# Tying TensorE's order in two attention branches of a decoder trunk, with stick-breaking values in pairs

## The chip, the cores and the metric

The kernel runs on one core of a Trainium2 chip. The metric is the device time of one execution in microseconds (us). A core has five engines that matter here: TensorE (PE in the rows, its weight loads PEld), VectorE (DVE), ScalarE (ACT), GpSimd (POOL) and SyncE (SP), which issues DMAs. Each has a queue of its own and works it off in the order in which it was written; semaphores tie the queues together.

## The reference, cut to what matters

One layer of a decoder trunk over 1024 tokens of 1024 channels in float32: a token mixer of three gated attention branches, then a feed-forward network with a short convolution.

```python
def banded_attention(q, k, v, bias, mask):      # branches A and B, per block of 128 queries, 256 keys
    logits = jnp.einsum('nkgbqd,nkbsd->nkgbqs', qb, kw) * SCALE
    logits = jnp.where(mask, logits + bias[:, :, None], -jnp.inf)
    m = jnp.max(logits, axis=-1)
    p = jnp.exp(logits - m[..., None])
    l = jnp.sum(p, axis=-1)
    num = jnp.einsum('nkgbqs,nkbsd->nkgbqd', p, vw)

def stick_breaking_attention(q, k, v):          # branch C, per block of queries
    z = jnp.einsum('bhqd,bhsd->bhqs', q, k) * SCALE
    log_keep = jnp.where(before, jax.nn.log_sigmoid(-z), 0.0)
    log_rest = lax.cumsum(log_keep, axis=3, reverse=True) - log_keep
    wts = jnp.where(before, jnp.exp(jax.nn.log_sigmoid(z) + log_rest), 0.0)
    out = jnp.einsum('bhqs,bhsd->bhqd', wts, v)
...
merged = g0 * (o_a @ w_br_a) + g1 * (o_b @ w_br_b) + g2 * (o_c @ w_br_c)
```

Branch A is dilated: three groups of heads with dilations 1, 4 and 16, whose results are combined per token by their softmax denominators. Branch B is a sliding window with a sink per head.

## The kernel before, in words

The input projection, the feed-forward's first product and its last are done by seven block products instead of eight, with float32 operands split into two parts and three matmuls each (`mm3_steps`, line 133). Between the input projection and the output projection lies the stretch that matters here, from about 578 to 905 us of the profile.

*Banded branches A and B.* `att_AB` (line 805) gives four stages for a pair of query blocks. `scores` (line 812) makes the logits on TensorE (`mm_qk`, lines 719 and 720), VectorE adds the bias and takes the maximum in one reduction (line 826), and ScalarE the exponentials (line 879 for A, 977 for B). `settled` lets ScalarE scale B's probabilities (line 986). `transposed` turns the probabilities on TensorE (line 845) and VectorE copies them out of PSUM (line 847). `values` multiplies them by the values (line 859): outputs of 64 rows, so the matmuls use one half of the array's columns for each head. The loop at line 1150 has 24 rounds; A has 24 pairs of blocks (6 units of 4), B has 16. In round k it traces transposes of A(k), scores of A(k + 2), transposes of B(k), scores of B(k + 2), values of A(k), values of B(k). From k = 16 A is alone. `combine` (line 918) joins A's dilated groups: small VectorE operations, then transposes (line 941) and six broadcast products (line 949) through a PSUM bank with the tag "cum". It runs beside the loop from k = 12 for the first pair of heads.

*Stick-breaking branch C.* `att_C` (line 723) has 40 steps of two heads, 128 keys and up to 256 queries. `logits` of step n + 3 (line 736) are followed by a chain over VectorE, ScalarE and GpSimd (lines 744 to 755). `weights` adds the step to the running sum in the bank "cum" (line 763); VectorE subtracts it (line 764) and ScalarE exponentiates. `carry` (line 771) prepares the sum for the next step; it must wait until VectorE has read. `values` (line 778) makes two 64-column products into the bank "o", and ScalarE copies that out at the end of a group of steps (line 783). In each round the trace has carry(n - 1), weights(n), then a yield, then values(n - 1) and logits(n + 3), then a yield.

At each yield the main loop (line 1172) puts in 11/9 steps of `fill` (three matmuls of line 137 each): the projections of branches B and A by `branch` (line 1011), each with a product by the gate on VectorE (lines 1034 and 1036), and the loads and splits of the output weights. The second `combine` runs beside it, a step at each yield.

*What sets the order.* The program is written with tiles; its scheduler takes the traced instructions and writes each engine's queue from when it expects them to be ready. So a queue is not always in the order of the text. Shared banks set the order too: "d" (three banks) for logits, "z" (two) for transposes and fill, "oab", "o" and "cum" (one each).

Of the kernel before, what the change touches and what calls it, by code (L numbers as in the profile page):

```python
# [72 lines left out]
def decoder_kernel(ctx, tc, x, rel_bias, attn_pre, w_in, b_gate, sinks, w_br_a, w_br_b, w_br_c,  # L73
# [290 lines left out]
    nc.tensor.transpose(ps[:, :KT], grow, ident[:KT, :KT])  # L364
# [12 lines left out]
    def to_channels(grp, k):  # L377
        ps = bank_z("ps_xT")
        for i in range(4):
            nc.tensor.transpose(ps[:, i * P : i * P + P], xts[4 * grp + i][:, k * P : k * P + P], ident)  # L380
        return ps
# [70 lines left out]
    def init_vectors():  # L452
# [14 lines left out]
        for i in range(3):  # L467
            n = 24 if i == 0 else P
            ps = bank_z("ps_vec")
            nc.tensor.transpose(ps[:, :n], vrow[:n, i, :], ident[:n, :n])  # L470
            nc.vector.tensor_copy(pvec[:, i, :n], ps[:, :n])

        nc.vector.memset(table[NBUCKET : NBUCKET + 1, :], 1.0)
        for s in range(4):
            h0, nh = 4 * s, (4 if s < 3 else 8)
            ps = bank_z("ps_rv")
            nc.tensor.matmul(ps[:nh, :384], table[:, h0 : h0 + nh], oh[:, s, :], start=True, stop=True)
# [55 lines left out]
    def keep_v(c, u, r):  # L533
        dil = dil_of(c)
        if T // dil < P:
            by_r = hst["b"][:, r, 1, :]
            nc.scalar.copy(by_r.rearrange("p (r l) -> p r l", r=dil), by_residue(u, dil))
            u, dil = by_r, 1
        v = hst["b"][:, r, 0, :].rearrange("p (i c) -> p i c", i=NB)
        for n in range(2):  # L540
            ps = bank_z("ps_v")
            for i in range(4):
                b = 4 * n + i
                r, l = divmod(b * P, T // dil)
                t0 = dil * l + r
                nc.tensor.transpose(ps[:, i * P : i * P + P], u[:, t0 : t0 + dil * (P - 1) + 1 : dil], ident)
            nc.vector.tensor_copy(v[:, 4 * n : 4 * n + 4, :], ps.rearrange("p (i c) -> p i c", i=4))
        nc.gpsimd.dma_start(v_d[VS.index(c)], v)
# [168 lines left out]
    def mm_qk(z, q, k, kl, ss, ms):  # L717

        nc.tensor.matmul(z, q[:, ss], k[:, ms], start=True, stop=False)
        nc.tensor.matmul(z, q[:, ss], kl[:, ms], start=False, stop=True)  # L720


    def att_C():
# [6 lines left out]
        def logits(n):  # L730
# [3 lines left out]
            for hh in range(2):  # L734
                for m, x in enumerate(("k", "kl")):
                    nc.tensor.matmul(z[:, hh, c0:], uC[p][j // 4][x][hh][:, j % 4 * P : j % 4 * P + P],  # L736
                                     uC[p][c // 2]["q"][hh][:, 256 * (c % 2) + c0 : 256 * (c % 2) + 256],
                                     start=m == 0, stop=m == 1 and j < 2 * c)
                if j >= 2 * c:
                    nc.tensor.matmul(z[:, hh, c0 : c0 + P], negd[:, 0, :], negd[:, 1, :], start=False, stop=True)  # L740
# [17 lines left out]
        def weights(n, p, c, j, c0, z, sp):  # L758
# [3 lines left out]
            for m, part in enumerate(sp):  # L762
                nc.tensor.matmul(cum, Lm, part, start=m == 0 and j == 2 * c + 1, stop=True, skip_group_check=True)
# [4 lines left out]
        def carry(n, p, c, j, c0, z, sp):  # L768
            if j > 0:
                for part in sp:  # L770
                    nc.tensor.matmul(banks["cum"][:, :, c0:], NLm, part, start=False, stop=True, skip_group_check=True)

        def values(n, p, c, j, c0, z, sp, w):
# [3 lines left out]
            for hh in range(2):  # L777
                nc.tensor.matmul(o[HR[hh], c0:256], uC[p][j // 4]["v"][:, j % 4, HR[hh]], w[:, hh], start=(j == 2 * c + 1), stop=(j == 0),  # L778
                                 skip_group_check=True)
# [9 lines left out]
        for n in range(len(steps)):  # L789
# [4 lines left out]
            if n > 0:  # L794
                values(n - 1, *live[n - 1], ws_[n - 1])
# [5 lines left out]
        values(n, *live[n], ws_[n])  # L801
# [3 lines left out]
    def att_AB(u, vcol, bias, banded, own, negm, soften, done, otag):  # L805
# [32 lines left out]
        def transposed(n):  # L838
# [3 lines left out]
            for hh in range(2):  # L842
                ps = psz.tile([P, 4, P], F32, tag="z", name="ps_pT")
                for m, (b, c) in enumerate(slots):
                    nc.tensor.transpose(ps[:, m, :], prs[hh][:, b, c * P : c * P + P], ident)  # L845
# [5 lines left out]
        def values(n):  # L851
# [4 lines left out]
            for m, (b, c) in enumerate(slots):  # L856
                i, nch = 2 * n + b, ws[b] // P
                for hh in range(2):
                    nc.tensor.matmul(o[HR[hh], (i % 4) * P : (i % 4) * P + P],  # L859
                                     u["v"][:, i - (nch - 1) + c, vcol(hh) : vcol(hh) + 64], pTs[hh][:, m, :],  # L860
                                     start=(c == 0), stop=(c == nch - 1))
# [56 lines left out]
    def combine(p):  # L918
# [226 lines left out]

    for k in range(2):
# [28 lines left out]
    for _ in fill:  # L1175
        pass
    raws_c = load_branch(w_br_c)
# [57 lines left out]
    def residual(tt, ys):  # L1235
# [22 lines left out]
        for kh in range(2):  # L1258
            ps = bank_e("ps_hT") if tt == NB - 1 else bank_d("ps_hT")
            for k in range(4):  # L1260
                nc.tensor.transpose(ps[:, k * P : k * P + P], y[:, (4 * kh + k) * P : (4 * kh + k + 1) * P], ident)
# [104 lines left out]
    def down_product(banks, make, start, stagger=0, side=iter(())):  # L1366


        def step(kk, e, hl, ms):
            sh, th = hl  # L1370
            for m in ms:
                for n, (a, b) in enumerate(PASSES):
                    f0 = kk == 0 and e == 0 and n == 0
                    nc.tensor.matmul(banks[m], sh[:, a, m * P : m * P + P], th[:, b], start=start and f0,  # L1374
                                     stop=kk == NK - 2 and e == 1 and n == 2, skip_group_check=not start)
# [173 lines left out]
```

## Time and profile before

| what | value |
|---|---|
| runs (3) | median 1950.8 us, 1949.98 to 1953.85 |
| the profiled execution | 1950.72 us, span 1948.9 us |
| mean granted TensorE clock | 0.991 of full speed |
| TensorE, VectorE, ScalarE, GpSimd busy | 96%, 73%, 52%, 15% of the span |
| chain that ended last | 69% TensorE, 9% VectorE, 9% issue, 7% DMA |

The span goes from the first to the last instruction; the execution's time has 1.8 us more. Busy time is the union of an engine's instructions. TensorE's matmuls overlap one another: each row's duration is longer than the time until the next matmul starts, so what a matmul costs is read from the starts of the timeline. In a row of the timeline, "x4" says that four instructions of one form follow each other; a bracket gives the idle time of the engine before the row and what ended it. A value product appears as two records.

### The profile page before, as it was taken

To read this page: it belongs to the slowest core of one execution; us is meant where nothing else is said; L and a number is where in the kernel's file an instruction comes from. 1 tells how busy PE (TensorE), PEld (TensorE's weight loads), DVE (VectorE), ACT (ScalarE), POOL (GpSimd) and SP (SyncE) were. 2 spreads that over 40 slices of the span, in tenths; PEclk is the share of its full clock that TensorE was granted. 3 is DMA by queue.
4 is the path that set the end of the run, shared out by engine and by line. 5 is a ranking of instruction groups with operands and counts; after the bars stand their busy time and mean duration, and the time that the engine had idled before them with its cause. 6 is when DMAs were issued, how large, how long until landed. Compare 5 with 4: busy or idle time off the path is not lost.

```text
span 1948.9 us, 24575 instructions
## 1 busy us (share of the span) xinstructions
PE 1878.8 (96%) x8904; PEld 1513.3 (78%) x8904; DVE 1425.5 (73%) x2280; ACT 1011.9 (52%) x1903; POOL 292.7 (15%) x333
## 2 busy tenths in 40 slices
PE   6899999999999999999989999999999999999997
PEld 4788887788887766767877888888888888878875
DVE  7866655445538879797588877878787875599896
ACT  6644433344449966773455554545455454445443
POOL 4212200100011003374150000000000000010122
PEclk9999999999999999999999999999999999999999
DMA  4487743643358542344223322222232217686572
GB/s 153 137 232 204 217 129 105 211 151 111 106 209 268 201 150 92 108 128 170 93 71 109 96 76 87 78 85 87 76 97 76 87 55 266 221 315 225 183 261 94
DMA packets 220409, 283.57 MB, mean 146 GB/s; under 512 B 14639, under 2 KB 145725, under 8 KB 220288
## 3 DMA queue, kind: packets, MB, share of 16 engines
q1 hardware_dynamic: 197168, 202.03, 32.2%
q0 software_dynamic: 22960, 79.90, 12.6%
q8 instruction: 70, 1.15, 0.2%
q14 instruction: 51, 0.42, 0.1%
q10 hardware_dynamic: 160, 0.07, 0.0%
HBM read 207.94 MB, written 77.95 MB: 147 GB/s over the span
## 4 chain that ended last, share of the span: by engine, by line
PE 69%; issue 9%; DVE 9%; DMA 7%; ACT 3%; POOL 2%; SPq 0%; DVEq 0%; POOLq 0%; ACTq 0%
PE st_a L137 26%; PE st_c L137 12%; PE e L1374 6%; PE st_b L137 6%; PE ps_y L137 4%; PE d L1374 3%; PE ps_b L137 3%; PE o_ab L859 2%; PE ps_pT L845 1%; DMA rep_d<-rv_d 1%; PE z_c L736 1%; DVE bT L120 1%; DMA rc<-g_d 1%; DMA ra<-g_d 1%; PE o_c L778 1%
## 5 line engine op out<-in xcount | busy, mean ns | idle before, releaser
L137 PE MATMUL st_a<-bT,w_hl 128*128 128x512 f32 x2124 | 514.9, 392 | 9.1 <-DVE mixbuf L128 3.1
L137 PEld LDWEIGHTS st_a<-bT,w_hl 128*128 128x128 f32 x2124 | 401.1, 189 | 96.5 <-DVE mixbuf L128 3.5
L118 ACT ACTIVATE w_hl<-w_raw 128x512 fp32r<-128x512 f32 x236 | 147.4, 630 | 295.6 <-PE st_c L137 171.6
L1374 PE MATMUL e<-th,sh 128*128 128x512 f32 x912 | 216.0, 390 | 2.7 <-DVE th L120 2.6
L118 ACT ACTIVATE w_hl<-s 128x512 fp32r<-128x512 f32 x177 | 111.6, 633 | 195.4 <-PE st_a L137 176.1
L120 DVE TENSOR_TENSOR w_hl<-w_raw,w_hl 128x512 fp32r<-128x512 f32 x236 | 165.7, 705 | 60.3 <-ACT w_hl L118 60.2
L1374 PEld LDWEIGHTS e<-th,sh 128*128 128x128 f32 x912 | 170.9, 188 | 39.9 <-DVE th L120 4.0
L120 DVE TENSOR_TENSOR w_hl<-s,w_hl 128x512 fp32r<-128x512 f32 x177 | 122.9, 696 | 88.4 <-ACT w_hl L118 88.3
L137 PE MATMUL st_a<-b,w_hl 128*128 128x512 f32 x708 | 180.9, 401 | 4.5 <-DVE w_hl L120 4.0
L1325 DVE SCALAR_TENSOR_TENSOR ybuf<-ubuf,pvec,ybuf 128x1023 f32<-128x1023 f32 (+1 forms) x128 | 163.8, 1281 | 21.0 <-ACT ybuf L1323 19.9
L137 PE MATMUL st_b<-b,w_hl 128*128 128x512 f32 x708 | 171.5, 390 | 0.0
L137 PE MATMUL st_c<-bT,w_hl 128*128 128x512 f32 x708 | 170.6, 389 | 0.0
L137 PE MATMUL st_c<-b,w_hl 128*128 128x512 f32 x684 | 164.7, 389 | 0.0
L137 PEld LDWEIGHTS st_a<-b,w_hl 128*128 128x128 f32 x708 | 134.8, 193 | 34.1 <-DVE w_hl L120 4.7
L137 PEld LDWEIGHTS st_c<-bT,w_hl 128*128 128x128 f32 x708 | 133.0, 188 | 27.8 <-ACT w_hl L118 0.2
L137 PEld LDWEIGHTS st_b<-b,w_hl 128*128 128x128 f32 x708 | 132.9, 188 | 27.6
L137 PEld LDWEIGHTS st_c<-b,w_hl 128*128 128x128 f32 x684 | 128.6, 188 | 27.0 <-ACT ubuf L247 0.2
L1374 PE MATMUL d<-th,sh 128*128 128x512 f32 x432 | 107.3, 391 | 3.1 <-DVE th L120 3.0
L137 PE MATMUL ps_b<-o_hl,wb_hl 128*128 128x512 f32 x384 | 105.2, 399 | 4.5 <-DVE gate L1036 2.9
L1330 POOL DMA_DIRECT2D g_d<-ybuf x32 | 17.1, 535 | 591.8 <-DVE ybuf L1329 591.8
L1374 PEld LDWEIGHTS d<-th,sh 128*128 128x128 f32 x432 | 80.7, 188 | 21.9 <-DVE th L120 5.1
L137 PE MATMUL ps_y<-wo,m_hl 128*128 128x512 f32 x384 | 88.8, 391 | 0.0
(273 smaller groups left out, 2934.5 us busy)
## 6 DMA issues: line engine op xcount, KB each, us to landing
w_raw<-in_w_up_dram SPq DMA_DIRECT2D x65, 512.0 KB, 4.2
w_raw<-in_w_in_dram SPq DMA_DIRECT2D x54, 512.0 KB, 5.2
ra<-g_d SPq DMA_DIRECT2D x40, 512.0 KB, 4.5
rb<-in_w_down_dram SPq DMA_DIRECT2D x40, 512.0 KB, 4.8
k_d<-hst POOLq DMA_DIRECT2D x36, 512.0 KB, 7.2
g_d<-ybuf POOLq DMA_DIRECT2D x32, 512.0 KB, 2.9
gate_d<-mixbuf POOLq DMA_DIRECT2D x24, 512.0 KB, 4.4
gate<-gate_d SPq DMA_DIRECT2D x48, 256.0 KB, 3.6
```

The costliest lines, as they stand in the source:

```text
L118: nc.scalar.activation(hi, src, AF.Copy, scale=scale)
L120: nc.vector.tensor_tensor(lo, src, hi.bitcast(F32), op=ALU.subtract)
L137: nc.tensor.matmul(ps, st(a, k), mv(b, k), start=start and n == 0, stop=stop and n == 3 * nk - 1, **kw)
L736: nc.tensor.matmul(z[:, hh, c0:], uC[p][j // 4][x][hh][:, j % 4 * P : j % 4 * P + P], uC[p][c // 2]["q"][hh][:, 256 * (c % 2) + c0 : 256 * ...
L778: nc.tensor.matmul(o[HR[hh], c0:256], uC[p][j // 4]["v"][:, j % 4, HR[hh]], w[:, hh], start=(j == 2 * c + 1), stop=(j == 0), skip_group_ch ...
L845: nc.tensor.transpose(ps[:, m, :], prs[hh][:, b, c * P : c * P + P], ident)
L859: nc.tensor.matmul(o[HR[hh], (i % 4) * P : (i % 4) * P + P], u["v"][:, i - (nch - 1) + c, vcol(hh) : vcol(hh) + 64], pTs[hh][:, m, :], sta ...
L1325: nc.vector.scalar_tensor_tensor(y[:, d:], src[:, : T - d], cw[2 - d][:, c : c + 1], y[:, d:], op0=ALU.mult, op1=ALU.add)
L1330: nc.gpsimd.dma_start(g_d[f * P : f * P + P, :], ys[0])
L1374: nc.tensor.matmul(banks[m], sh[:, a, m * P : m * P + P], th[:, b], start=start and f0, stop=kk == NK - 2 and e == 1 and n == 2, skip_grou ...
```

## The change

Between `ordered = True`, ahead of the first scores of A and B, and `ordered = False`, behind the last fill, each TensorE instruction is tied behind the one that was traced before it on TensorE. No semaphore is added, only the order in the queue is set. In the stick-breaking branch the values of two steps are traced together, in the rounds with even n. The second `combine` uses the bank "oab", which the banded branches leave, in place of "cum".

```diff
+    ordered = False
+
+    def pe(ins):
+
+        return tc.keep_in_program_order(ins) if ordered else ins
...
-                nc.tensor.matmul(ps, st(a, k), mv(b, k), start=start and n == 0, stop=stop and n == 3 * nk - 1, **kw)
+                pe(nc.tensor.matmul(ps, st(a, k), mv(b, k), start=start and n == 0, stop=stop and n == 3 * nk - 1, **kw))
...
@@ -791,14 +797,16 @@
                 carry(n - 1, *live[n - 1])
             ws_.append(weights(n, *live[n]))
             yield
-            if n > 0:
-                values(n - 1, *live[n - 1], ws_[n - 1])
+            if n > 0 and n % 2 == 0:
+                for m in (n - 2, n - 1):
+                    values(m, *live[m], ws_[m])
             if n + 3 < len(steps):
                 live.append(logits(n + 3))
             if steps[n] == (0, 3, 2):
                 load_C(1, 1, uC[1][1])
             yield
-        values(n, *live[n], ws_[n])
+        for m in (n - 1, n):
+            values(m, *live[m], ws_[m])
...
         for n in range(2):
-            ps = pso.tile([P, 512], F32, tag="cum", name="ps_w")
+            ps = pso.tile([P, 512], F32, tag=("cum", "oab")[p], name="ps_w")
             for i in range(4):
-                nc.tensor.transpose(ps[:6, i * P : i * P + P], cg[:, 4 * n + i].rearrange("a g h -> a (g h)"), ident)
+                pe(nc.tensor.transpose(ps[:6, i * P : i * P + P], cg[:, 4 * n + i].rearrange("a g h -> a (g h)"), ident))
...
-                pw = pso.tile([P, 512], F32, tag="cum", name="pw")
-                nc.tensor.matmul(pw, sel[:, g, :], wT, start=True, stop=True)
+                pw = pso.tile([P, 512], F32, tag=("cum", "oab")[p], name="pw")
+                pe(nc.tensor.matmul(pw, sel[:, g, :], wT, start=True, stop=True))
...
+    ordered = True
     for k in range(2):
         sa.scores(k)
         sb.scores(k)
...
     for _ in fill:
         pass
+    ordered = False
     raws_c = load_branch(w_br_c)
```

The same `pe(...)` stands around all other calls on TensorE in these functions (lines 719, 720, 736, 740, 763, 771, 778, 845 and 859). `keep_in_program_order` adds an edge to the queue's previous instruction and returns the instruction. Outside the stretch `pe` returns its argument.

## Rows read from the trace of the kernel before

**Rows 1.** Part 1 of the page: busy time, share, instructions.

```profile
PE 1878.8 (96%) x8904; PEld 1513.3 (78%) x8904; DVE 1425.5 (73%) x2280; ACT 1011.9 (52%) x1903; POOL 292.7 (15%) x333
```

**Rows 2.** Windows: stretch, us; busy PE, PEld, DVE, ACT, POOL; clock, DMA share, GB/s.

```profile
583.00:665.00 82.00, 78.76 (x689) 63.69 (x689) 67.86 (x321) 77.29 (x289) 7.08 (x12) 1.00 0.72 244
665.00:694.00 29.00, 27.99 (x222) 20.31 (x221) 24.89 (x98) 22.73 (x82) 1.43 (x2) 1.00 0.40 136
694.00:717.00 23.00, 22.12 (x193) 17.31 (x190) 19.29 (x83) 15.24 (x57) 1.35 (x2) 1.00 0.63 191
717.00:755.00 38.00, 35.52 (x182) 24.64 (x180) 31.65 (x50) 23.88 (x48) 9.96 (x9) 1.00 0.39 126
755.00:820.00 65.00, 65.00 (x345) 46.33 (x344) 52.90 (x85) 47.94 (x94) 21.57 (x18) 1.00 0.27 87
820.00:881.00 61.00, 56.56 (x273) 36.83 (x271) 59.35 (x79) 41.94 (x77) 43.56 (x30) 1.00 0.44 143
881.00:905.00 24.00, 20.79 (x88) 15.74 (x87) 21.00 (x24) 6.18 (x8) 17.46 (x15) 1.00 0.82 292
```

**Rows 3.** TensorE's timeline in the banded stretch: start, duration, work.

```profile
645.41 1.09 PE L859 MATMUL o_ab<-pT,v 128*64 128x128 f32 x14
646.43 0.39 PE L719 MATMUL z_ab<-b_qk 128*128 128x256 f32 x1
...
646.77 0.29 PE L719 MATMUL z_ab<-b_qk 128*128 128x256 f32 x1
646.90 0.28 PE L720 MATMUL z_ab<-b_qk 128*128 128x256 f32 x1
647.10 0.43 PE L859 MATMUL o_ab<-pT,v 128*64 128x128 f32 x2
647.47 0.33 PE L719 MATMUL z_ab<-qk 128*128 128x128 f32 x1
```

**Rows 4.** The same timeline: first and last of 72 visits of line 859.

```profile
583.81 0.43 PE L859 MATMUL o_ab<-pT,v 128*64 128x128 f32 x2
...
716.06 1.09 PE L859 MATMUL o_ab<-pT,v 128*64 128x128 f32 x14
```

**Rows 5.** TensorE's timeline in the stick-breaking branch.

```profile
772.18 0.65 PE L778 MATMUL o_c<-zs,v 128*64 128x256 f32 x4
772.77 0.73 PE L736 MATMUL z_c<-q,k 128*128 128x256 f32 x4
773.34 0.86 PE L137 MATMUL ps_b<-o_hl,wb_hl 128*128 128x512 f32 x3
774.06 0.50 PE L771 MATMUL cum<-sp,tri 128*128 128x256 f32 x2
...
774.87 0.86 PE L137 MATMUL ps_b<-o_hl,wb_hl 128*128 128x512 f32 x3
775.66 0.44 PE L778 MATMUL o_c<-zs,v 128*64 128x128 f32 x4
776.03 0.74 PE L736 MATMUL z_c<-q,k 128*128 128x256 f32 x4
```

**Rows 6.** Waits (us, times, longest): ScalarE 583 to 665, TensorE 820 to 881.

```profile
ACT o_hl L118 <- PE o_ab L859: 2.4, 5, 1.1
...
PE cum L771 <- DVE zs L125: 1.7, 4, 0.8
```

**Rows 7.** VectorE by line, 694 to 717 us: count, busy, mean ns, idle before.

```profile
L847 DVE COPY pT<-ps_pT 128x256 f32<-128x256 f32 (+2 forms) x15 | 7.7, 544 | 3.0 <-PE ps_pT L845 3.0
L826 DVE CUSTOM_DVE_ANT_0 s_ab<-z_ab,bias 128x256 f32<-128x256 f32 (+1 forms) x24 | 7.5, 363 | 0.0
```

**Rows 8.** TensorE's timeline, 717 to 755 us: rows with idle time.

```profile
722.20 0.50 PE L763 MATMUL cum<-sp,tri 128*128 128x256 f32 x2 [0.67 <-DVE wT L943]
...
725.28 0.50 PE L771 MATMUL cum<-sp,tri 128*128 128x256 f32 x2 [1.18 <-DVE zs L125]
...
744.13 0.60 PE L941 MATMUL ps_w<-ident,cg 128*6 128x128 f32 x4 [0.63 <-DVE zs L125]
```

More of the change, by code (lines that the diff above doesn't have):

```diff
@@ L363, in decoder_kernel @@
     ps = bank_z("ps_g0")
-    nc.tensor.transpose(ps[:, :KT], grow, ident[:KT, :KT])
+    pe(nc.tensor.transpose(ps[:, :KT], grow, ident[:KT, :KT]))
     nc.vector.tensor_copy(g_attn, ps[:, :KT])
@@ L379, in to_channels @@
         for i in range(4):
[L380 removed]
+            pe(nc.tensor.transpose(ps[:, i * P : i * P + P], xts[4 * grp + i][:, k * P : k * P + P], ident))
         return ps
@@ L476, in init_vectors @@
             ps = bank_z("ps_rv")
-            nc.tensor.matmul(ps[:nh, :384], table[:, h0 : h0 + nh], oh[:, s, :], start=True, stop=True)
+            pe(nc.tensor.matmul(ps[:nh, :384], table[:, h0 : h0 + nh], oh[:, s, :], start=True, stop=True))
             rv = buf[:nh, 2560 + 384 * s : 2560 + 384 * s + 384]
@@ L717, in mm_qk @@
     def mm_qk(z, q, k, kl, ss, ms):
-        nc.tensor.matmul(z, q[:, ss], k[:, ms], start=True, stop=False)
-        nc.tensor.matmul(z, q[:, ss], kl[:, ms], start=False, stop=True)
+        pe(nc.tensor.matmul(z, q[:, ss], k[:, ms], start=True, stop=False))
+        pe(nc.tensor.matmul(z, q[:, ss], kl[:, ms], start=False, stop=True))
     def att_C():
@@ L762, in weights @@
             for m, part in enumerate(sp):
-                nc.tensor.matmul(cum, Lm, part, start=m == 0 and j == 2 * c + 1, stop=True, skip_group_check=True)
+                pe(nc.tensor.matmul(cum, Lm, part, start=m == 0 and j == 2 * c + 1, stop=True, skip_group_check=True))
             sub(w, z, cum)
@@ L770, in carry @@
                 for part in sp:
-                    nc.tensor.matmul(banks["cum"][:, :, c0:], NLm, part, start=False, stop=True, skip_group_check=True)
+                    pe(nc.tensor.matmul(banks["cum"][:, :, c0:], NLm, part, start=False, stop=True, skip_group_check=True))
         def values(n, p, c, j, c0, z, sp, w):
@@ L777, in values @@
             for hh in range(2):
-                nc.tensor.matmul(o[HR[hh], c0:256], uC[p][j // 4]["v"][:, j % 4, HR[hh]], w[:, hh], start=(j == 2 * c + 1), stop=(j == 0),
-                                 skip_group_check=True)
+                pe(nc.tensor.matmul(o[HR[hh], c0:256], uC[p][j // 4]["v"][:, j % 4, HR[hh]], w[:, hh], start=(j == 2 * c + 1), stop=(j == 0),
+                                 skip_group_check=True))
             if j == 0:
@@ L858, in values @@
                 for hh in range(2):
-                    nc.tensor.matmul(o[HR[hh], (i % 4) * P : (i % 4) * P + P],
+                    pe(nc.tensor.matmul(o[HR[hh], (i % 4) * P : (i % 4) * P + P],
                                      u["v"][:, i - (nch - 1) + c, vcol(hh) : vcol(hh) + 64], pTs[hh][:, m, :],
-                                     start=(c == 0), stop=(c == nch - 1))
+                                     start=(c == 0), stop=(c == nch - 1)))
             if n % 2 == 1:
@@ L1373, in step @@
                     f0 = kk == 0 and e == 0 and n == 0
-                    nc.tensor.matmul(banks[m], sh[:, a, m * P : m * P + P], th[:, b], start=start and f0,
-                                     stop=kk == NK - 2 and e == 1 and n == 2, skip_group_check=not start)
+                    pe(nc.tensor.matmul(banks[m], sh[:, a, m * P : m * P + P], th[:, b], start=start and f0,
+                                     stop=kk == NK - 2 and e == 1 and n == 2, skip_group_check=not start))
         held = []
```

14 lines of the change are left out of this document (7 added, 7 removed).

## The prediction

> **What bounds the kernel now.** Part 1 of the page comes first: TensorE is busy for 1878.8 of 1948.9 us [rows 1]. A matmul's row is longer than the time until the next may start, so a busy share of 96% does not say that the array is full; for that the starts are needed. Next the stretch that the change touches is cut into seven windows [rows 2]. In the first 82 us of the banded attention ScalarE is busy for 77.29 us, that is 94%: the exponentials and scalings set the pace, and TensorE, at 78.76 us, has little more to spare. From 665 to 694 us, where the first combination of the dilated groups runs beside it, ScalarE falls to 22.73 of 29 us and TensorE is at 27.99. From 694 to 717 us only the dilated branch is left: TensorE 22.12, VectorE 19.29, ScalarE 15.24 of 23. In the stick-breaking branch TensorE has no gap from 755 to 820 us (65.00 of 65), and from 820 to 881 us VectorE is the bound with 59.35 of 61. A saving on TensorE is therefore worth different sums in these windows.
>
> Last the order of TensorE's work is read from its timeline. In the banded stretch the value products (line 859) do not stand together: a visit of two records, then logits, transposes, another visit [rows 3]. From the first to the last of them [rows 4] I count 72 visits: 41 before 665 us, 18 from there to 694 us, 13 after. The text of the program asks for 24 groups: 16 in which both branches' values follow each other, and 8 of the dilated branch alone. In the stick-breaking branch TensorE already runs as the text says: values, logits, fill, carry, weights, fill, values [rows 5]. So tying the order changes much in the first part and little in the second.
>
> **What a visit costs.** Fourteen records take 646.43 - 645.41 = 1.02 us to the next product, two take 647.47 - 647.10 = 0.37 us [rows 3]. That is 0.054 us a record and 0.26 us for the visit itself. Going in costs too: the logits product before a visit holds the engine for 647.10 - 646.90 = 0.20 us, one with logits behind it for 0.13 us, so 0.07 us. A visit costs 0.33 us beyond its work. Changes between transposes and logits I set at nothing, since the one way gains about what the other loses.
>
> **The banded stretch to 694 us.** 59 visits become 16; 43 times 0.33 is 14.2 us of TensorE's time. Not all of it can come back, because ScalarE is next. In the first window ScalarE idles 82 - 77.29 = 4.7 us, and 2.4 us of that is its copy of finished outputs waiting for the last value product [rows 6]; tied order doesn't take that wait away. I take 1 us there. From 665 to 694 us the 18 visits become 4, which is 4.6 us, and ScalarE has 6.3 us to spare; I take 4 us. **Term: -5 us.** Bounds: 4.7 + 4.6 = 9.3 us gained; at the other end 3 us lost, if TensorE waits in its new order for probabilities that ScalarE gives late, by the idle 2.4 us of [rows 6] and a little more.
>
> **The dilated branch alone, 694 to 717 us.** 13 visits become 8, a gain of 1.7 us. Against it stands a new wait. In tied order the queue is transposes(k), scores(k+2), values(k), and values need the copies of both transposed tiles (line 847). Behind the waiting product stands everything of TensorE, the next logits first, on which VectorE and then ScalarE live. A copy takes 0.544 us [rows 7]; two come to 1.1 us, and since the first begins while the second half is still being transposed I take 1 us for both. For k = 16 to 21 eight logits products of 0.13 us [rows 3] cover that, unless VectorE first works off up to four reductions of 0.363 us and their read-outs [rows 7]: 0 to 1.8 us a round; I take 0.3, together 1.8 us. For k = 22 and 23 there are no scores left and nothing covers: 2 us. In the old order the first logits of the stick-breaking branch and its fill stood there. **Term: +2 us.** Bounds: -1.7 with no wait, +11 with all of them (2 + 6 times 1.8 - 1.7).
>
> **The start of the stick-breaking branch.** Before, the second combination borrows the bank of the running sum, and weights wait for it: 0.67 us at 722.20, 1.18 us at 725.28 and 0.63 us at 744.13 [rows 8] are TensorE's whole idle time from 717 to 755 us, 38 - 35.52 = 2.5 us [rows 2]. With the bank "oab" this conflict goes. But the combination's chain is now tied into the queue: each of its six broadcast products needs the bank back from VectorE's multiplication (an estimate of 0.7 us with its hand-over, from the copy's 0.544 us [rows 7]), and its transposes need the small VectorE chain. Also the branch's first logits now start behind the last values, not 8 us before them. **Term: 0**, between -2.5 (idle time gone) and +4.2 (six waits of 0.7 us).
>
> **Values of two steps together.** Full-width values take 772.77 - 772.18 = 0.59 us, half-width 776.03 - 775.66 = 0.37 us [rows 5]; half the columns cost 0.22 us, so 0.59 - 0.44 = 0.15 us is the visit. Going in: three fill products before values take 775.66 - 774.87 = 0.79 us, before a carry 774.06 - 773.34 = 0.72 us. A visit costs 0.22 us, and 20 of 40 go: 4.4 us. Only the window where TensorE is the bound can give it back, some 20 steps between 755 and 820 us, so 10 visits: 2.2 us. After 820 us VectorE's 59.35 us are the same work [rows 2]. The step moves no DMA and no output copy: each pair ends where the single one did, and the logits' buffer that is read longer is refilled only by logits that stand behind in the same queue. What it takes away is cover: in the odd rounds some 0.6 us of values no longer stand between weights and the next carry, which waits for VectorE's subtraction. That wait is 1.7 us in four places now [rows 6]. The even rounds give the same back, so I set it at nothing; if seven odd rounds lose all of it, it is +4 us. **Term: -2 us**, from -4.4 to +2.
>
> [...]
>
> **Sum.** -5 + 2 + 0 - 2 = -5 us. The profiled execution took 1950.72 us (span 1948.9), 0.1 us off the median of 1950.8; the forecast is 1945.7, said as 1946 us. Nothing after 905 us is touched by the diff; I let it shift. About 0.2%, or 3.9 us, is what a measurement of this kernel can tell from no change, so this forecast lies just on the faster side of that line.
>
> **Rivals.** *The wait for the copies decides (slower).* Place: values behind their transposes, in the banded stretch. Price: if both copies lie open in each of 24 groups, 24 times 1.1 us = 26 us, less 48 visits or 15.8 us, less 2 us of the pairs: +8 us, 1959 us. It decides once the open wait passes (15.8 + 2)/24 = 0.74 us a group. For it: the old order broke the values up just where the copies were late, and VectorE works 83% of that stretch [rows 2]. Against it: scores of the same round stand between, and in 16 of 24 rounds those of two branches. [...]
>
> *ScalarE and VectorE hide it (no change).* The banded stretch stays at ScalarE's pace, the lone branch loses 2 us, the pairs give 2: 1950 us. For it: ScalarE's 94% in the first window and VectorE's 97% from 820 us [rows 2]. A form of it is that the tie does nothing in the stick-breaking branch, which already runs so.
>
> *TensorE is the true bound (much faster).* All 15.8 us and 4.4 us come back: 1931 us. Against it: ScalarE has only 11 us idle before 694 us.
>
> **Chances.** The forecast's case has 0.50 (own range 1938 to 1951): 0.32 beyond the line, since its centre lies there and its terms reach further down than up, 0.13 within 0.2%, 0.05 slower. The slower rival has 0.20, all of it slower. No change has 0.20, of which 0.04 for a gain over the line. The much faster case has 0.10. Faster by over 0.2%: 0.32 + 0.04 + 0.10 = 0.46; the same 0.13 + 0.16 = 0.29; slower 0.05 + 0.20 = 0.25. The range goes from 1934 us, which leaves out the far end of the large gain, to 1958 us, just short of the slower rival's middle.
>
> **What would show it.** Right: some 24 value visits in the banded stretch, runs of 32 records, TensorE's sum of busy time there down by over 10 us while ScalarE's share rises over 94%; the stretch shorter by about 5 us to 694; in the stick-breaking branch eight value records in a row, 20 times, and no wait of weights on the combination. The lone branch not shorter. Wrong: value products that wait for pT by over 0.7 us each; carries that wait for VectorE in odd rounds; a gain that is gone by 905 us; or a stretch after 905 us that changes its length.

## The result and the profile after

| | median | lowest to highest | ratio to before, 95% interval |
|---|---|---|---|
| before | 1950.39 us | 1948.01 to 1953.85 | |
| changed | 1963.13 us | 1957.72 to 1964.53 | 1.0056 [1.0041, 1.0070] |

The change makes the kernel slower by half a per cent, outside the range that was given. (The ratio is not the quotient of the two medians, which would be 1.0065.) The profiled execution of the changed kernel took 1957.72 us (span 1955.9), 7.0 us more than the one of before. It is the shortest of the six; the medians are 12.7 us apart, so the 7.0 us that are followed up below are not all of the difference.

Part 1 of the page, which answers to [rows 1]:

```profile
PE 1864.8 (95%) x8904; PEld 1515.9 (78%) x8904; DVE 1427.4 (73%) x2280; ACT 1011.3 (52%) x1903; POOL 292.3 (15%) x333
```

The instructions are the same in number on every engine. TensorE is busy 14 us less and the kernel is longer: time went from work into waiting.

**Where it went.** Four landmarks are read from TensorE's timeline, each by the start of its product: the first banded logits, the last value product of branch B, the last of branch A, and the last of the stick-breaking branch.

| stretch | before | changed | difference | predicted term |
|---|---|---|---|---|
| first banded logits to B's last values | 116.1 us | 121.3 us | +5.2 | -5 |
| from there to A's last values | 22.8 us | 23.8 us | +1.0 | +2 |
| from there to the last stick-breaking values | 163.9 us | 162.5 us | -1.4 | 0 - 2 |

That is +4.8 of the 7.0 us. The rest lies in stages that the diff doesn't touch; the largest part of it is the last product of the feed-forward, 3.2 us longer in this profile. The first stretch is the failure. Its windows, in the changed kernel (columns as in [rows 2]):

```profile
583.00:665.00 82.00, 68.91 (x627) 60.56 (x626) 62.93 (x295) 70.77 (x267) 6.31 (x11) 0.89 0.71 238
583.00:594.00 11.00, 7.38 (x41) 6.30 (x41) 7.25 (x37) 9.68 (x40) 3.50 (x7) 0.66 1.00 362
594.00:612.00 18.00, 16.44 (x159) 14.83 (x157) 13.27 (x64) 15.06 (x57) 0.71 (x1) 0.88 0.72 252
612.00:665.00 53.00, 45.09 (x434) 39.43 (x433) 42.42 (x198) 46.02 (x172) 2.10 (x3) 0.94 0.64 208
```

ScalarE, which set the pace with 77.29 of 82 us [rows 2], is busy for 70.77 now. So nothing came off its work; it is given work too late. And a column that said 1.00 in every row of before says 0.66, 0.88 and 0.94: TensorE was at half clock for part of each window. Cut finer, the granted clock of the changed kernel is 0.50 in whole windows (582 to 584, 589 to 594, 606 to 608, 626 to 629 and 647 to 649 us) and 1.00 between them (595 to 605, 609 to 625, 630 to 645 us). So a mean of 0.66 in 11 us means 11 x 0.34 x 2 = 7.5 us at half clock; with 4.3, 6.4 and another 1.8 us just before 583 that is 20 us. Before, the stretch had none.

What TensorE waited for, from 577 to 723 us (us in all, times, longest):

```profile
PE ps_pT L853 <- ACT pr L994: 13.9, 9, 3.1
PE o_ab L867 <- ACT num L899: 1.5, 2, 0.8
PE ps_pT L853 <- DVE pT L855: 1.4, 2, 0.9
PE z_ab L725 <- DVE st L834: 1.3, 1, 1.3
PE o_ab L867 <- DVE pT L855: 1.1, 4, 0.6
...
```

One line holds most of the waiting: transposes of branch B (line 853, once 845) wait for line 994 (once 986), ScalarE's scaling of B's probabilities in `settled`. The wait for the copies of the transposed tiles, on which the slower rival was built, is the last line shown, 1.1 us.

The longest of these waits on ScalarE's timeline, in the changed kernel (start, duration, work, idle time before):

```profile
587.56 0.51 ACT L985 ACTIVATE pr<-s_ab,nm 128x256 f32<-128x256 f32 x1 [1.32 <-DVE nm L978]
...
589.15 0.49 ACT L985 ACTIVATE pr<-s_ab,nm 128x256 f32<-128x256 f32 x1
...
589.64 1.48 ACT L994 ACTIVATE pr<-pr,l 128x128 f32<-128x128 f32 x4
```

and the same place in the kernel before:

```profile
587.27 0.80 ACT L986 ACTIVATE pr<-pr,l 128x128 f32<-128x128 f32 x2
587.98 0.49 ACT L977 ACTIVATE pr<-s_ab,nm 128x256 f32<-128x256 f32 x1
...
590.04 0.78 ACT L986 ACTIVATE pr<-pr,l 128x128 f32<-128x128 f32 x2
```

In both kernels the scalings of round 0 stand in ScalarE's queue among or behind the exponentials of round 1. Before, two of the four ran at 587.27, and TensorE's queue held other work until the rest were done. In the changed kernel all four stand behind the exponentials, which themselves begin late. TensorE's timeline shows what the tied order does with that:

```profile
586.73 0.28 PE L726 MATMUL z_ab<-k,q 128*128 128x256 f32 x1
590.08 1.78 PE L853 MATMUL ps_pT<-ident,pr 128*128 128x128 f32 x6 [3.07 <-ACT pr L994]
591.51 0.56 PE L725 MATMUL z_ab<-b_qk 128*128 128x256 f32 x1
...
600.85 0.88 PE L853 MATMUL ps_pT<-ident,pr 128*128 128x128 f32 x6
601.48 0.30 PE L725 MATMUL z_ab<-qk 128*128 128x128 f32 x1
```

The transposes of B(0) are at the head of the queue and TensorE stands still for 3.07 us, from 587.01. What the scalings need was there long before they ran: VectorE finished their reciprocals (line 990, also part of `settled`) at 587.61 us.

```profile
587.44 0.17 DVE L990 RECIPROCAL l<-l 128x4 f32<-128x4 f32 x1
```

From there to 589.64 us ScalarE did exponentials that stand ahead in its queue: 2.03 of the 3.07 us are the place of the scalings, the rest is VectorE's reciprocal before and the first scaling behind. Behind the transposes are the logits of B(2), on which VectorE and then ScalarE live, so ScalarE runs dry a round later: its exponentials at 594.81 us wait 0.74 us for a maximum from VectorE, and from 583 to 665 us such waits are 4.5 us in four places, where they were 0.7 us in two before. And the six transposes take 591.51 - 590.08 = 1.43 us to the next product, where six take 601.48 - 600.85 = 0.63 us later; the granted clock is 0.50 from 589 to 594 us and 1.00 from 595 to 605. The half clock came with the wait.

What was predicted of the order itself did happen. The 72 visits of value products [rows 4] are 24 groups, such as 16 + 16 records at 661.79 and 662.72 us. The stick-breaking branch has its pairs (TensorE's timeline, beside [rows 5]):

```profile
776.72 1.08 PE L784 MATMUL o_c<-zs,v 128*64 128x256 f32 x8
777.74 0.74 PE L742 MATMUL z_c<-q,k 128*128 128x256 f32 x4
...
869.46 0.73 PE L777 MATMUL cum<-sp,tri 128*128 128x512 f32 x2 [2.58 <-DVE zs L125]
```

A pair takes 777.74 - 776.72 = 1.02 us where two single ones took 2 x 0.59 [rows 5]. The last row is the price in an odd round: a carry without values in front of it waits 2.58 us for VectorE.

### The profile page after: what moved, and what is told of

It reads as the page before. It is cut to its first block, busy times and chain, and to the rows that moved or that the text cites. A ratio compares the mean times of both kernels' runs of the same rounds, so it can differ in the third digit from the quotient of the medians.

```text
span 1955.9 us, 24570 instructions
## 1 busy us (share of the span) xinstructions
PE 1864.8 (95%) x8904; PEld 1515.9 (78%) x8904; DVE 1427.4 (73%) x2280; ACT 1011.3 (52%) x1903; POOL 292.3 (15%) x333
## 4 chain that ended last, share of the span: by engine, by line
PE 66%; DVE 11%; issue 10%; DMA 6%; ACT 5%; POOL 2%; SPq 0%; POOLq 0%; DVEq 0%; ACTq 0%
PE st_a L143 26%; PE st_c L143 13%; PE e L1384 7%; PE st_b L143 6%; PE ps_y L143 4%; PE d L1384 3%; PE ps_b L143 2%; DMA rep_d<-rv_d 1%; PE ps_pT L853 1%; ACT pr L985 1%; DMA rc<-g_d 1%; DVE bT L120 1%; PE o_ab L867 1%; DVE sh L120 1%; DMA rb<-in_w_down_dram 1%
## 5 line engine op out<-in xcount | busy, mean ns | idle before, releaser
L143 PEld LDWEIGHTS st_c<-bT,w_hl 128*128 128x128 f32 x708 | 132.9, 188 | 27.8 <-ACT w_hl L118 0.2
L143 PEld LDWEIGHTS st_b<-b,w_hl 128*128 128x128 f32 x708 | 132.9, 188 | 27.6
```

Of the source, the lines that this page charges most:

```text
L143: pe(nc.tensor.matmul(ps, st(a, k), mv(b, k), start=start and n == 0, stop=stop and n == 3 * nk - 1, **kw))
```

## The experiments

"Stretch" is the time from the first banded logits to A's last values, and behind the bar from there to the last stick-breaking values; "at half clock" is worked out from the windows as above. Before: 139.0 | 163.9 us, with none at half clock. Changed: 145.2 | 162.5, 20 us in the first. Diffs are against the changed kernel unless they say otherwise.

### One half of the tie each

The tie only from the stick-breaking branch on (with pairs and the other bank):

```diff
-    ordered = True
     for k in range(2):
...
+    ordered = True
     sc, fill = stream_C(), fills()
```

> The tie begins only behind the banded branches; pairs and the bank oab stay. Theory W (the loss is the tied queue's wait in the banded stretch, where B's transposes stand behind ScalarE's scalings, with the half clock that follows): no such wait left, granted clock 1.00 from 578 to 700 us, 1946 to 1950 us. Rival C (the tie or the pairs cost time in the stick-breaking branch or behind it): 1955 us or more.

Measured: ratio 1.0005 [0.9992, 1.0018]; 138.1 | 163.0 us.

The tie only in the banded stretch, everything behind it as before:

```diff
-            if n > 0 and n % 2 == 0:
-                for m in (n - 2, n - 1):
-                    values(m, *live[m], ws_[m])
+            if n > 0:
+                values(n - 1, *live[n - 1], ws_[n - 1])
...
-            ps = pso.tile([P, 512], F32, tag=("cum", "oab")[p], name="ps_w")
+            ps = pso.tile([P, 512], F32, tag="cum", name="ps_w")
...
+    ordered = False
     sc, fill = stream_C(), fills()
```

> The tie ends before the stick-breaking branch, which is as before the change (single values, bank cum). Theory W: all of the loss remains, 1957 to 1965 us, the first value product again near 593 us and the last near 722 us. Rival C: 1948 to 1953 us.

Measured: 1.0036 [1.0021, 1.0051]; 145.8 | 164.4 us, 20 us at half clock. The wait is there again:

```profile
PE ps_pT L851 <- ACT pr L992: 14.5, 10, 3.4
```

So the loss lies in the banded half of the tie. The half in the stick-breaking branch, with all that goes with it, is worth nothing that can be measured.

### Take the wait away

B's probabilities are scaled a round earlier, so that ScalarE's queue has the scalings ahead of B's next exponentials; all of the change stays. `settled` moves as a whole, so VectorE's sum and reciprocal for the scalings come earlier too.

```diff
         sa.scores(k)
+        if k:
+            sb.settled(0)
         sb.scores(k)
...
-        if both:
-            sb.settled(k)
         sa.transposed(k)
...
         sa.scores(k + 2)
+        if k < 15:
+            sb.settled(k + 1)
```

> The changed kernel, but ScalarE's scalings of B's next pair are traced one round earlier, between the scores of A and of B, so that they stand before the exponentials of that round in ScalarE's queue. TensorE's order is the same. Theory W: the 13.9 us of waits of B's transposes go below 3 us, no half clock from 578 to 700 us, the banded stretch ends at 712 us or earlier, 1938 to 1948 us in all. If the waits go but the time doesn't (ScalarE is the bound), 1950 to 1956 us. Rival C: as the changed kernel, 1958 to 1964 us.

Measured: 0.9997 [0.9983, 1.0012]; 135.8 | 169.4 us. The wait on line 994 is gone, the stretch is 9.4 us shorter than in the changed kernel and ScalarE is full (window, same columns):

```profile
612.00:665.00 53.00, 47.12 (x476) 41.92 (x474) 47.41 (x226) 52.40 (x198) 2.82 (x4) 1.00 0.66 213
```

The time, 1952.65 us, is the one expected if ScalarE bounds the stretch. Theory W's 1938 to 1948 us were missed: 7 us at half clock are left in the stretch, which ends at 715 us and not at 712. What comes next in line are the waits for the output bank and for the first combination (us in all, times, longest), and in the stick-breaking branch a broadcast product of the second combination, which holds the queue for 3.11 us:

```profile
PE o_ab L867 <- ACT num L899: 4.4, 5, 1.6
PE ps_w L949 <- DVE cg L944: 2.6, 1, 2.6
```

That product on TensorE's timeline:

```profile
728.02 0.49 PE L957 MATMUL pw<-wT,sel 64*128 64x512 f32 x1 [3.11 <-DVE num L958]
```

The stick-breaking branch is 7 us longer than in the changed kernel, with some 14 us at half clock: in this profile, which at 1956.39 us lies above the median of its kernel, most of what the first stretch gained was given back in the second.

### The pairs alone

The changed kernel with single values (the first part of the diff of the second experiment).

> The changed kernel with single values in the stick-breaking branch. If the pairs give what the forecast's sum took: 2 to 4 us slower than the changed kernel, 1964 to 1967 us, and 4 us more from the first weights to the last value product. If the uncovered odd rounds cost as much: the same 1962 us. Rival C in the form that pairs harm: 1953 to 1958 us.

Measured: 1.0047 [1.0035, 1.0059]; 145.2 | 166.3 us. The pairs shorten the stick-breaking stretch of these profiles by 3.8 us, about half of it clock (3.4 us at half clock without them, none with them). The second profile of the changed kernel, below, has 3.4 us at half clock and 164.4 us, so that the pairs give 1.9 us there. The times differ by less than their intervals.

### Move what stands behind the wait

B's logits of round k + 2 go ahead of B's transposes.

```diff
         if both:
-            sb.transposed(k)
             sb.scores(k + 2)
+            sb.transposed(k)
```

> The changed kernel with B's scores of round k + 2 traced ahead of B's transposes of round k, so that 1.1 us of TensorE's work stands between A's scores and the waiting transposes, and ScalarE gets its next logits earlier. Theory W (order alone, no engine too slow): the wait of B's transposes falls from 13.9 us to 4 to 8 us and the time to 1950 to 1957 us. If ScalarE were simply too slow in this stretch, the wait would move to another product and the time stay at 1960 us or more.

Measured: 1.0040 [1.0026, 1.0054]; 142.2 | 164.3 us. The wait moved:

```profile
PE z_ab L725 <- DVE st L834: 7.1, 9, 1.4
PE o_ab L867 <- DVE pT L855: 5.3, 14, 1.3
...
PE ps_pT L853 <- ACT pr L994: 1.5, 2, 1.0
```

With transposes directly ahead of their values nothing covers the copies of the transposed tiles any more, and the logits wait for their buffers. Here the rival's wait does appear, 5.3 us in 14 places. In this fixed order, too, some input comes late.

### The clock's own share

The waits stay, but TensorE is kept at work in six of them by 85 products that nobody reads; no other work is added or left out.

```diff
+            spare = {0: 22, 2: 11, 5: 17, 6: 9, 8: 17, 10: 9}.get(k, 0)
+            if spare:
+                idle = pso.tile([P, 512], F32, tag="cum", name="idle")
+                for _ in range(spare):
+                    pe(nc.tensor.matmul(idle[:, :256], uB["k"][0][:, 0:P], uB["k"][0][:, 0:256], start=True, stop=True))
             sb.transposed(k)
```

> The changed kernel with idle products put ahead of the waiting transposes in rounds 0, 2, 5, 6, 8 and 10 (85 products of 256 columns whose output nobody reads, about 0.11 us each, 9 us in all, by the lengths of the waits). They remove no wait. Theory K (the half clock after the waits costs several us of its own): granted clock 1.00 from 578 to 665 us and 3 to 6 us faster than the changed kernel, 1957 to 1960 us. If the clock costs nothing, because TensorE waits anyway: 1962 us as the changed kernel, or up to 3 us slower.

The changed kernel once more, beside it on the same chip:

> The changed kernel once more, beside the others on the same chip. Every theory: ratio 1.004 to 1.007, the same waits of B's transposes (12 to 15 us) and half clock in at least three places between 578 and 665 us; it gives the baseline for the pairs, the order and the fill.

Measured: with the products 1.0036 [1.0022, 1.0049] and 140.5 | 168.4 us; the changed kernel again 1.0042 [1.0029, 1.0055] and 144.3 | 164.4 us, its wait 14.4 us in 9 places. With the products the windows read

```profile
583.00:594.00 11.00, 10.25 (x74) 9.10 (x74) 7.96 (x42) 9.47 (x40) 2.91 (x7) 0.84 1.02 371
594.00:612.00 18.00, 17.62 (x184) 15.67 (x179) 14.49 (x68) 16.95 (x65) 1.23 (x2) 1.00 0.73 253
612.00:665.00 53.00, 50.09 (x492) 43.95 (x491) 44.37 (x206) 48.26 (x182) 2.10 (x3) 1.00 0.64 208
```

0.84, 1.00 and 1.00, where 0.66, 0.88 and 0.94 stood; the 1.00 from 578 us on that was expected came only from 594. More work on TensorE made the stretch 3.8 us shorter (4.7 us against the first profile of the changed kernel). So of its +6.2 us some 4 are the clock's; by subtraction the remaining 2 are what the waits cost beyond the visits saved. The times do not show it: their intervals overlap, and this profile lost 4 us in the stick-breaking branch, with 10 us at half clock there.

### A second output bank

With early scalings, the largest wait left was for the output bank (line 899). Branch A's outputs take the bank of the running sum in five rounds, as the combination leaves it free. Diff against the kernel with early scalings:

```diff
-                bank["o"] = pso.tile([P, 512], F32, tag=otag, name="o_ab")
+                other = otag == "oab" and k in (2, 6, 10, 18, 22)
+                bank["o"] = pso.tile([P, 512], F32, tag="cum" if other else otag, name="o_ab")
```

> The kernel with the early scalings, and in addition the value products of A use the idle bank cum beside oab in rounds 2, 6, 10, 18 and 22, so that they don't wait for ScalarE's copy of the outputs before. If what is left in the banded stretch is that wait (4.4 us of ScalarE's copies and 2.3 us of VectorE's split in the kernel with early scalings): 2 to 4 us faster than that kernel, 1946 to 1950 us, ratio 0.997 to 0.999. If ScalarE bounds the stretch by then: no difference, ratio 0.999 to 1.001.

Measured: 1.0013 [1.0000, 1.0025]; 136.1 | 167.7 us. No gain. The wait on ScalarE's copies went, and waits on the same outputs' split on VectorE (line 120) rose from 2.3 to 5.5 us.

### Early scalings without the tie

The kernel before, as a control, and the kernel before with early scalings and nothing else (the diff of the third experiment, on the kernel before):

> The kernel before, once more, as a run among the others: how far two profiles and two medians of the same kernel lie apart. Ratio 0.999 to 1.001; banded stretch to its last value product within 1.5 us of the 716.6 us of the first profile; granted clock 1.00 there. If the half clock in this stretch came and went by chance, not with the tied order's waits, it would appear here too.

> The kernel before with nothing but the early scalings, no tie, no pairs. If the early scalings are a gain of their own (the scheduler had them late too): 2 to 4 us faster than before, ratio 0.998 or less. If they only undo what the tie exposed: ratio 0.999 to 1.001 here. Theory W expects the second, since TensorE's free order already went round that wait (0.5 us in one place).

Measured: the control 1.0002 [0.9990, 1.0014], 139.2 | 163.9 us. With early scalings 0.9961 [0.9945, 0.9976], 132.6 | 169.3 us. The second was a miss: early scalings were thought to mend only what the tie had broken, and they gain 7 us on the old order by themselves. ScalarE has 51.98 of 53 us in the stretch and the value products still come in 55 visits. Two windows:

```profile
612.00:665.00 53.00, 51.01 (x493) 42.86 (x490) 47.37 (x225) 51.98 (x196) 3.53 (x5) 1.00 0.61 195
...
718.00:729.00 11.00, 11.00 (x32) 6.08 (x31) 5.92 (x9) 5.26 (x10) 1.94 (x2) 0.53 0.15 48
```

and TensorE's timeline just ahead of the second:

```profile
717.78 0.50 PE L771 MATMUL cum<-sp,tri 128*128 128x256 f32 x2 [2.27 <-DVE zs L125]
```

The second window and this row show why its stick-breaking branch is longer: a carry waits 2.27 us, and the 11 us behind it run almost wholly at half clock. In this profile that takes back 5.4 of the 6.4 us; it is one execution, and it lies above the median of its kernel (1944.61 against 1942.22 us). It is 6.1 us shorter than the profile of before, but the two stretches give only 1.0 us of that; 2.3 us lie ahead of the first banded logits and 2.9 us behind the last stick-breaking value, where the edit touches nothing. So where the 7 us of the medians come from is shown only in part.

This kernel also changes what the third experiment says. Early scalings shorten the first stretch by 9.4 us with the tie (145.2 to 135.8) and by 6.4 us without it (139.0 to 132.6). Only the difference, some 3 of the tie's +6.2 us, belongs to the meeting of the tie with late scalings. The other 3 us are still there, as other waits, when the scalings are early (135.8 against 132.6), and so is much of the loss in time (0.9997 against 0.9961). These are single profiles; the two of the kernel before differ by 0.3 us in this stretch, the two of the changed kernel by 0.9.

### The tie with its waits mended

Early scalings, the tie in the banded stretch alone, pairs and the other bank kept, and one more `yield` after each small VectorE chain of the combination, so that its products stand later in the queue. Against the kernel with early scalings:

```diff
             nc.vector.tensor_tensor(cg[:, :, g, :], cg[:, :, g, :], den, op=ALU.mult)
         yield
+        yield
...
             nc.vector.tensor_tensor(wT[32:38], ps[:6], wT[0:6].bitcast(F32), op=ALU.subtract)
             yield
             yield
+            yield
...
+    ordered = False
     sc, fill = stream_C(), fills()
```

> Early scalings, the tie in the banded stretch alone, pairs and the bank oab kept but untied, and one more yield each ahead of the combination's transposes and of its broadcast products, so that the tied queue reaches them 1 to 2 us later. Theory W: the waits on the combination's small VectorE chain (2.55 and 1.45 us in the kernel with early scalings) go, the banded stretch is 2 to 5 us shorter than before the change; 1946 to 1950 us, ratio 0.997 to 0.999. If ScalarE bounds the stretch and the stick-breaking branch takes the rest: ratio 0.999 to 1.001.

Without that spacing, and with the stick-breaking branch as before (the second experiment with early scalings):

> Early scalings and the tie in the banded stretch alone; the stick-breaking branch as before the change. It differs from the second experiment only in the early scalings. Theory W: ratio lower than that one's 1.0036 by 0.003 to 0.006, that is 0.998 to 1.001, the wait of B's transposes on ScalarE below 3 us and at most two places of half clock in the banded stretch. If the loss of the second experiment had another cause: 1.003 or more.

Measured: spaced 0.9958 [0.9944, 0.9972], 133.3 | 161.2 us; not spaced 0.9994 [0.9982, 1.0007], 135.7 | 164.0 us. The first, with 1941.9 us, is better than was expected of it. The second still waits for the combination:

```profile
PE o_ab L865 <- ACT num L897: 4.6, 5, 1.7
PE ps_w L947 <- DVE cg L942: 2.5, 1, 2.5
...
PE pw L955 <- DVE wT L949: 1.6, 1, 1.6
```

### Is the tie worth anything at all?

Three kernels on one chip: the spaced kernel without any tie; with the whole tie of the change; and with the banded tie, but single values.

```diff
-    ordered = True
     for k in range(2):
         sa.scores(k)
```

> The kernel e10 (early scalings, pairs, oab, later combination products) with the tie of the banded stretch taken out. If the tie gains by the 48 visits saved, as the forecast's sum took: slower than e10 by 3 to 6 us, ratio 0.997 to 0.999. If ScalarE bounds the stretch and the visits are worth nothing: the same as e10, 0.995 to 0.997. If the tie costs even then: 0.994 or less. I expect the second.

```diff
-    ordered = False
     sc, fill = stream_C(), fills()
```

> The changed kernel with its full tie, early scalings and later combination products; it differs from e3 (ratio 0.9997) by those products alone. If the tied queue's wait on the combination's chain is what was left: 3 to 6 us faster than e3, ratio 0.996 to 0.998, and the waits of the combination's transposes and products below 1 us each. If the tie of the stick-breaking branch is what was left: no better than 0.999.

> The kernel e10 with single values. If the pairs give 2 us as the forecast's sum took: slower than e10 by 1 to 3 us, ratio 0.9965 to 0.998, and the stretch from the last banded value to the last stick-breaking one 164 us in place of 161 us. If they give nothing: 0.995 to 0.9965 and 161 us.

| kernel | median | ratio to before | stretch |
|---|---|---|---|
| no tie, early scalings, spaced, pairs | 1937.61 us | 0.9933 [0.9919, 0.9948] | 130.9, 162.4 us |
| whole tie | 1944.27 us | 0.9961 [0.9949, 0.9974] | 132.3, 160.7 us |
| banded tie, single values | 1943.90 us | 0.9964 [0.9953, 0.9975] | 133.2, 162.8 us |

The first was a miss: it was expected level with the tied one, and it is the fastest kernel of the study, 14.7 us below the 1952.28 us of before in that comparison. Against early scalings alone (0.9961) it has the pairs, the bank and the spacing in addition; which of them gives the rest was not run by itself. Its value products come in 55 visits; the spaced kernels with the tie have 24 or 25. One window shows what some 30 visits are worth to ScalarE: no tie first,

```profile
612.00:665.00 53.00, 51.61 (x497) 43.33 (x498) 47.35 (x225) 52.54 (x199) 3.52 (x5) 1.00 0.61 198
```

then the whole tie:

```profile
612.00:665.00 53.00, 47.39 (x487) 41.99 (x486) 47.37 (x226) 52.31 (x199) 3.18 (x5) 1.00 0.62 203
```

The tie takes 51.61 - 47.39 = 4.2 us of TensorE's busy time away, as fewer visits should, and ScalarE does no more work for it: it is at 99% either way. In the first stretch the tie costs 1.4 us here (132.3 against 130.9). Its waits stand there (4.5 us for the output bank, 3.1 us for copies), and some 3 us at half clock that the untied kernel has not in that stretch.

Yet the 6.7 us between these two medians are not in the stretches: together they take 293.3 us without the tie and 293.0 us with it. The two profiles are 6.3 us apart elsewhere: 1.9 us ahead of the first banded logits, 3.4 us from the last stick-breaking value to the last product of the output projection, 1.3 us in the feed-forward's last product. The 3.4 us go with the tie. Every profile with the stick-breaking branch tied has 117.4 to 119.9 us there, every one without 114.8 to 116.8; before it is 116.8, in the changed kernel 118.2. No run tells how.

The kernel with the whole tie also shows what was wrong with early scalings and the tie without spacing: spaced, it goes from 0.9997 to 0.9961, so that loss was the combination's place in the queue, with the half clock behind it (14 us in the stick-breaking branch, none here). Single values cost 1.6 us of stretch against pairs (162.8 against 161.2), within the intervals of the times.

## Why the prediction was wrong

**The step that failed is the term of the banded stretch to 694 us, -5 us, and in it the bound "3 us lost, if TensorE waits in its new order for probabilities that ScalarE gives late".** It came out at +5.2 us. The wait was named and its engine was right, but it was sized by the 2.4 us of [rows 6], and that is a wait the other way: ScalarE's, for TensorE's value products. TensorE's own wait for the scalings was, before (577 to 723 us; us, times, longest),

```profile
PE ps_pT L845 <- ACT pr L986: 0.5, 1, 0.5
```

and that could not bound it either, since it belongs to an order that the scheduler had made so that such waits hardly arise. In the new order it is 13.9 us in 9 places. Some 3 of the stretch's +6.2 us go with it, by the runs with and without early scalings. The other 3 do not. Where this wait is gone the tied queue waits for the output bank and for the first combination's small VectorE chain (4.4 us, and 2.6 and 1.5 us), and the chain had no term in the banded stretch either; with the combination's products later in the queue the tie still costs 1.4 us.

That the wait would be long could have been read from the trace of before: the text puts B's transposes of round k directly behind A's logits of k + 2, and ScalarE's timeline shows two scalings of round 0 at 587.27 and two at 590.04, behind exponentials of round 1. That both orders, TensorE's new one and ScalarE's old one, meet at this place was not looked at; only VectorE's copies were.

**The visits.** Their number (24) was right, and the price of 0.33 us about right: over the first stretch of the two spaced kernels TensorE is busy for 125.9 us with 55 visits and for 115.8 us with 24, that is 0.33 us a visit if all that the tie saves is put down to them. In the changed kernel it is busy for 122.4 us in place of 132.9, a fall of over 10 us, which the prediction had named as a sign of being right; the stretch grew all the same. The step from there to the time was weak: with ScalarE at 94% the text allowed a gain of up to what ScalarE had idle. The spaced kernels with early scalings fill ScalarE to 99%, with 55 visits as with 24, so that idle time was owed to the scalings' place in the queues. (Early scalings also bring the untied kernel from 72 visits to 55; what that does by itself was not tried.)

**The clock.** It had no term. In the trace of before the granted clock is 1.00 in all windows read [rows 2]; that a new wait also slows what runs after it made some 4 of the 6.2 us, by the run with idle products. These 4 us and the 3 us above are no parts of one sum, since the half clock comes with the waits.

**The dilated branch alone, +2 us:** +1.0 us. The size was nearly right, the reason only in part: the waits are for the output bank (0.70, 0.84 and 0.80 us at 707, 712 and 718 us) and a gap of 0.93 us that no release explains at 701; the copies of the last round's tiles add 0.60 and 0.16 us at 721 us.

**The start of the stick-breaking branch and the pairs, 0 and -2 us:** together -1.4 us in the first profile of the changed kernel, and +0.5 us in the second, with 3.4 us at half clock. The bank conflict of [rows 8] went, and two broadcast products wait 1.4 us instead. The pairs are worth 1.6 us with the rest mended and 1.9 or 3.8 us in the changed kernel, near the 2 us of the sum. The uncovered carries came as bounded: 4.1 us in 6 places, 2.58 us the longest, against 2.9 us in 5 places before.

**The rivals.** The slower one gave 1959 us, which is 4 us from the result. That is luck, for the runs refute its reason: its wait was 1.1 us in the changed kernel. Logits between transposes and values covered the copies, as the text had said against it; the experiment with B's logits first, which takes that cover away, brings the wait out. The no-change rival had the right bound (ScalarE hides what TensorE saves), and the much faster one is refuted by the same rows.

**Open** stays the part of the 7.0 us outside these stretches. The prediction let all that lies behind 905 us shift as it is, and that did not hold. Of it, 1.4 us lie in the output projection and go with the tie of the stick-breaking branch, as said above. The largest part, 3.2 us, lies in the feed-forward's last product, which comes some 740 us after the tie ends. It goes with the banded tie all the same, and most with the late scalings: the product takes 315.6 to 317.5 us in all six profiles with the banded tie and late scalings, 313.8 to 314.8 us with the tie and early scalings, and 313.1 to 313.4 us without that tie, the control included. No run tells its cause. The start of the banded stretch varies too, from 574.3 to 581.3 us, by 3.7 us between the two profiles of the kernel before. Open is also how often the half clock comes in the stick-breaking branch: profiles of kernels that differ only in the banded stretch have from 0 to 14 us of it.

## What to carry to other kernels

Before an engine's queue is tied to the program's order, lay the new order beside the queue of each engine that feeds it: at every tied instruction the question is whether its input stands early enough in the other queue, and the waits of the old order do not tell that. Move the late producer first (here the scalings, by one round, worth 7 us alone); then see whether the tie still gains anything. Here, with ScalarE at 99%, it did not. Spacing of small chains (a `yield` more between a VectorE chain and the product that reads it) is part of a tied order's price.

## What the runs showed of the hardware that had not been expected

- A wait of 3.07 us on TensorE was followed by work at half clock: the granted clock was 0.50 from 589 to 594 us, and six transposes took 1.43 instead of 0.63 us to the next product. In the stick-breaking branch a wait of 2.27 us was followed by 11 us with a granted clock of 0.53, although TensorE shows no gap in them (11.00 of 11.00 us busy). A wait of that length does not always have this effect: the carry's wait of 2.58 us at 869 us in the changed kernel left the granted clock at 1.00 from 820 to 881 us, and the three fill products behind it took 0.78 us to the next product; after 2.54 us at the same carry they took 1.41 us in that kernel's second profile and in the kernel with early scalings.
- 13.9 us of waits in nine places came with 20 us at half clock in a stretch where TensorE is busy 84% of the time (68.91 of 82 us).
- 85 products that nobody reads, put into six of those waits, brought the granted clock back to 1.00 from 594 to 665 us and shortened the stretch by 3.8 to 4.7 us.
